# Seven block products in a down projection: a two-layer transformer trunk on TensorE

## The chip, the cores and the metric

The kernel runs on one core of a Trainium2 chip. The metric is the device time of one execution in microseconds (us). Before the change the median of three runs is 2252.79 us (2252.79 to 2252.91). The profile is of one more execution.

The engines by the profile's names: PE is TensorE (matmuls), PEld its loading of stationary operands, DVE is VectorE, ACT is ScalarE, POOL is GpSimd, SP is SyncE, whose queue carries the DMA transfers.

## The reference

The input is 256 tokens by 2048 features, in float32. Each of two layers does, with weights of its own:

```python
h = rms_norm(x, pre_mix_norm[l])
m = hybrid_mixer(h, l, w_in[l], w_o[l], ...)      # two kinds of attention, 8 heads each
x = x + rms_norm(m, post_mix_norm[l])
h = rms_norm(x, pre_ffn_norm[l])
f = (silu(h @ w_gate) * (h @ w_up)) @ w_down      # 2048 -> 5632 -> 2048
x = x + rms_norm(f, post_ffn_norm[l])
```

All weights together are some 400 MB, each used once per execution.

## The kernel before, in words

**Precision.** A float32 matmul is made of three matmuls in fp32r: each operand is split into a rounded part `hi` and a rest `lo`, and hi x hi, hi x lo and lo x hi are summed in PSUM. One matmul is a stationary 128 x 128 block (tokens) against 128 x 512 columns of weights.

**Weights.** They come in a fixed list `stream` of transfers of 512 KB, each a *K pair*: two blocks of 128 rows by 512 columns, in a tile `raw` (4 buffers). `feed` (L167) splits each: ScalarE rounds `hi` (L177), VectorE subtracts for `lo` (L179), 6 buffers each, up to LOOKAHEAD = 4 transfers ahead of their use.

**Gate and up.** Eleven chunks of 512 columns, each over 8 K pairs. For 5 of the 8, the two blocks of tokens (t), two of K and the two matrices (gate and up) give 8 block products, 24 matmuls. For pairs 2, 4 and 6 (in the first chunk 4 and 6) a 2 x 2 by 2 x 2 block product is made with 7 products, 21 matmuls. For that, `mixed_weights` (L145) makes four sums of weight blocks (L151, tiles `T`) on VectorE, rounds them on ScalarE (L160, `Th`), subtracts on VectorE (L162, `Tl`), and also splits one plain block (b22, L155 and L156). The tokens' sums (`token_sums`, L703 to L716: two `f` of hi + lo, four small sums `s`, a rounded `sh` on ScalarE and a rest `sl`) are made once per layer, for all three pairs, ahead of the first chunk's K loop. Four PSUM banks hold the chunk's results (`c`); four more hold products that several results share (`p`, `q`). These are added on VectorE at the chunk's end (L779 to L791), then silu and the product; the result is transposed on TensorE some ticks later (`flip`) into tiles `act`.

**Down.** Two halves of the output columns, each two blocks of 512 (c). The K loop has 22 pairs; a pair is two transfers, one for each c, and 24 matmuls (L840, L841, L843) into four banks `dn`. `prep` (L814) splits the pair's activations into `jh` (ScalarE, L820) and `jl` (VectorE, L822), up to two pairs ahead. In half 1 the last 3 pairs (TAIL) are done per t and c (L862 to L864), so that the first tokens finish early. `evac_chunk` (L363) squares a bank on ScalarE for the norm (L365) and multiplies it with the gain on VectorE (L369); `rescale` (L371) makes the factor and updates x (L377). In layer 0 `transposed` (L290) then makes the next layer's input `xI`; in layer 1 the result is stored.

**Order.** A scheduler fixes each engine's order of instructions when the kernel is built, from the program's order, priorities (URGENT for the evacuation) and data dependences. At run time an engine takes its list in that order and waits for semaphores. `tick` counts steps of the program; generators such as `flip` and the attention advance on ticks. Tiles live in pools; a pool that is released gives its room to later ones, whose first writers wait for the last readers.

Of the kernel before, what the change touches and what calls it, by code (L numbers as in the profile page):

```python
# [9 lines left out]
F32 = mybir.dt.float32  # L10
F32R = mybir.dt.float32r
# [6 lines left out]
P = 128  # L18
# [19 lines left out]
FIRST_ORDER = (0, 1, 3, 2, 4, 5, 6, 7)  # L38

# [12 lines left out]
def kernel(  # L52
# [51 lines left out]
    for l in range(L):  # L104
# [102 lines left out]
    rows0 = const.tile([32, P], F32, name="rows0")  # L207
    rows = const.tile([64, P], F32, name="rows")
# [23 lines left out]
    lams = const.tile([P, 4, L * 64], F32, name="lams")  # L232
    negones = const.tile([P, P], F32, name="negones")
# [6 lines left out]
    def late_constants():  # L240
# [18 lines left out]
        lprod = const.tile([P, 2, L * 64], F32, name="lprod")  # L259
        lsum = const.tile([P, 2, L], F32, name="lsum")  # L260
# [53 lines left out]
    def x_tiles(nm):  # L314
        return [wpool.tile([P, 2, S], F32R, tag="xT", bufs=KT, name=f"{nm}_{k}") for k in range(KT)]
# [47 lines left out]
    def evac_chunk(pool, acc, mg, ssm, gpost, c, t, nm, mpool=None):  # L363
        junk = pool.tile([P, CW], F32, tag="t2", name=f"jm_{nm}_{t}_{c}")
        nc.scalar.activation(junk, acc, AF.Square, accum_out=ssm[t][:, c : c + 1])  # L365
        if c % 2 == 0:
            mg[t, c // 2] = (mpool or pool).tile([P, 2, CW], F32, tag="qk", bufs=4, name=f"mg_{nm}_{t}_{c}")
# [206 lines left out]
    def mixer_in(pool, l, rs, xT, mix, mixed):  # L574
        st = None
        for n, c in enumerate(plan[l]["chunks"]):
# [21 lines left out]
            if n == 0:  # L598
                if l == 0:
                    with tc.issue_after(marks[0].ins), tc.issue_after(marks[1].ins), in_turn():  # L600
                        late_constants()
                        rs = [inv_rms(t, pool, "in0") for t in range(NT)]
# [38 lines left out]
    def load_gain(pool, v, nm):  # L641
# [3 lines left out]
        return gp  # L645

    xT = None
    for l in range(L):
# [52 lines left out]
        def token_sums(kp):  # L701

# [4 lines left out]
            a11, a21, a12, a22 = f[:, 0, 0:P], f[:, 0, P:S], f[:, 1, 0:P], f[:, 1, P:S]  # L707
            s = pool.tile([P, 4, P], F32, tag="t2", name=f"s{l}_{kp}")
            nc.vector.tensor_tensor(out=s[:, 0, :], in0=a21, in1=a22, op=ALU.subtract)
            nc.vector.tensor_tensor(out=s[:, 1, :], in0=s[:, 0, :], in1=a11, op=ALU.subtract)  # L710
            nc.vector.tensor_tensor(out=s[:, 2, :], in0=a11, in1=a21, op=ALU.subtract)
            nc.vector.tensor_tensor(out=s[:, 3, :], in0=s[:, 1, :], in1=a12, op=ALU.add)
            sh = gu.tile([P, 4, P], F32R, tag="sh", bufs=len(SEVEN), name=f"sh{l}_{kp}")
            nc.scalar.activation(sh, s, AF.Copy)
            sl = gu.tile([P, 4, P], F32R, tag="sl", bufs=len(SEVEN), name=f"sl{l}_{kp}")
            nc.vector.tensor_tensor(out=sl, in0=s, in1=sh.bitcast(F32), op=ALU.subtract)  # L716
            forms[kp] = (sh, sl)

        def product(a, stat, moving, first, last):
            sh, sl = stat  # L720
            hi, lo = moving
            nc.tensor.matmul(a, sh, hi, start=first, stop=False)  # L722
            nc.tensor.matmul(a, sh, lo, start=False, stop=False)  # L723
            nc.tensor.matmul(a, sl, hi, start=False, stop=last)  # L724
# [11 lines left out]
        def seven(banks, extra, c, kp, first, last):  # L736
# [3 lines left out]
            sh, sl = forms[kp]  # L740
            s1, s2, s3, s4 = ((sh[:, j, :], sl[:, j, :]) for j in range(4))
            p1, p6, p7, q5 = extra
            todo = (
                (p1, (e[:, 0, 0:P], e[:, 1, 0:P]), (hi[:, 0, :], lo[:, 0, :]), first, last),
                (banks[0], (o[:, 0, 0:P], o[:, 1, 0:P]), (hi[:, 1, :], lo[:, 1, :]), False, False),
                (q5, s1, m["t1"], first, last),
                (p7, s3, m["t3"], first, last),
                (p6, s2, m["t2"], first, last),
                (banks[1], s4, m["b22"], False, False),
                (banks[2], (o[:, 0, P:S], o[:, 1, P:S]), m["t4"], False, False),  # L750
            )
            for n, job in enumerate(todo):
                if n % 2 == 0:
                    tick()
                product(*job)

        for c in range(FF // CW):
# [3 lines left out]
            if c == 0:  # L761
# [3 lines left out]
                for kp in SEVEN:  # L765
                    token_sums(kp)
                order = order[2:]
            extra = None
            for kp in order:
# [6 lines left out]
                if kp == mine[-1]:  # L776
                    p1, p6, p7, q5 = extra
                    w = [pool.tile([P, CW], F32, tag="t2", name=f"w{j}_{l}_{c}") for j in range(4)]
                    nc.scalar.copy(w[0], p1)  # L779
                    nc.vector.tensor_tensor(out=w[1], in0=p6, in1=w[0], op=ALU.add)  # L780
                    nc.vector.tensor_tensor(out=w[2], in0=p7, in1=w[1], op=ALU.add)
                    nc.vector.tensor_tensor(out=w[1], in0=q5, in1=w[1], op=ALU.subtract)
                    nc.vector.tensor_tensor(out=w[3], in0=q5, in1=w[2], op=ALU.subtract)  # L783
# [18 lines left out]
        gu.release()  # L802
        dn = tc.alloc_tile_pool(name=f"dn{l}", bufs=4, reuse_waits="tile")
# [108 lines left out]
```

## Time and profile before

| | |
|---|---|
| median of three runs | 2252.79 us |
| profiled execution | 2252.42 us |
| its span (first to last instruction) | 2250.7 us |
| TensorE | 10210 matmuls and transposes, busy 99% |
| VectorE, ScalarE | busy 72%, 54% |
| transfers | 421.62 MB, 187 GB/s over the span |

In layer 0, gate and up run from about 420 to 887 us and down from 887 to 1128 us. Layer 1's first gate/up chunk is near 1550 us, and its last matmul begins at 2241.87 us.

A row of a timeline has the start, the duration, the engine, the line, the operation, output <- inputs, shapes and a count; in brackets the idle time before it and what ended it. Busy times of matmuls overlap, since a new one starts before the last has left the pipe: the distance between starts is the price of one. The same holds for VectorE, whose rows back to back overlap by some 0.09 us.

### The profile page before, as it was taken

To read this page: it belongs to the slowest core of one execution; us is meant where nothing else is said; L and a number is where in the kernel's file an instruction comes from. 1 tells how busy PE (TensorE), PEld (TensorE's weight loads), DVE (VectorE), ACT (ScalarE), POOL (GpSimd) and SP (SyncE) were. 2 spreads that over 40 slices of the span, in tenths; PEclk is the share of its full clock that TensorE was granted. 3 is DMA by queue.
4 is the path that set the end of the run, shared out by engine and by line. 5 is a ranking of instruction groups with operands and counts; after the bars stand their busy time and mean duration, and the time that the engine had idled before them with its cause. 6 is when DMAs were issued, how large, how long until landed. Compare 5 with 4: busy or idle time off the path is not lost.

```text
span 2250.7 us, 28018 instructions
## 1 busy us (share of the span) xinstructions
PE 2225.4 (99%) x10210; PEld 1833.5 (81%) x10210; DVE 1626.3 (72%) x2225; ACT 1222.4 (54%) x1834; POOL 37.6 (2%) x76
## 2 busy tenths in 40 slices
PE   8999999999999999999999999999999999999998
PEld 6888888788888888888887888887888888888886
DVE  6666555899989988555576665559998998975555
ACT  6545555665555546444465555546655555554443
POOL 1010000000000000000010000000000000000000
PEclk9999999999999999999999999999999999999999
DMA  7555555475665666556565555554666566565553
GB/s 238 180 169 163 163 182 184 127 229 187 204 206 188 199 209 208 189 188 204 171 195 175 162 167 161 186 186 141 205 200 209 190 199 205 190 218 192 191 198 135
DMA packets 216699, 421.62 MB, mean 187 GB/s; under 512 B 13200, under 2 KB 13808, under 8 KB 216048
## 3 DMA queue, kind: packets, MB, share of 16 engines
q1 hardware_dynamic: 216560, 419.83, 58.2%
q8 instruction: 80, 1.31, 0.2%
q14 instruction: 59, 0.48, 0.1%
HBM read 417.68 MB, written 2.10 MB: 187 GB/s over the span
## 4 chain that ended last, share of the span: by engine, by line
PE 92%; DVE 3%; ACT 2%; DMA 2%; issue 0%; POOL 0%; SPq 0%; DVEq 0%; ACTq 0%
PE c L722 10%; PE c L723 10%; PE c L724 10%; PE in L358 8%; PE in L360 7%; PE in L359 7%; PE dn L843 7%; PE dn L840 7%; PE dn L841 7%; PE o L360 2%; PE o L358 2%; PE o L359 2%; PE p L724 2%; PE p L723 2%; PE p L722 2%; DVE lo L179 1%
## 5 line engine op out<-in xcount | busy, mean ns | idle before, releaser
L179 DVE TENSOR_TENSOR lo<-raw,hi 128x1024 fp32r<-128x1024 f32 x720 | 873.6, 1227 | 329.8 <-ACT hi L177 324.5
L177 ACT ACTIVATE hi<-raw 128x1024 fp32r<-128x1024 f32 x720 | 749.5, 1056 | 469.1 <-PE in L360 166.5
L722 PE MATMUL c<-hi,xF 128*128 128x512 f32 x960 | 377.8, 394 | 2.0 <-DVE w L783 1.6
L724 PE MATMUL c<-hi,xF 128*128 128x512 f32 x960 | 374.2, 391 | 0.0
L723 PE MATMUL c<-lo,xF 128*128 128x512 f32 x960 | 373.6, 390 | 0.0
L840 PE MATMUL dn<-hi,jh 128*128 128x512 f32 x656 | 255.6, 390 | 0.0
L841 PE MATMUL dn<-lo,jh 128*128 128x512 f32 x656 | 255.2, 389 | 0.0
L722 PEld LDWEIGHTS c<-hi,xF 128*128 128x128 f32 x960 | 180.6, 188 | 39.1 <-DVE w L783 2.5
L724 PEld LDWEIGHTS c<-hi,xF 128*128 128x128 f32 x960 | 180.4, 188 | 37.8
L723 PEld LDWEIGHTS c<-lo,xF 128*128 128x128 f32 x960 | 180.5, 188 | 36.3
L843 PE MATMUL dn<-hi,jl 128*128 128x512 f32 x656 | 202.1, 389 | 0.0
L160 ACT ACTIVATE Th<-T 128x1024 fp32r<-128x1024 f32 x128 | 135.2, 1056 | 116.9 <-DVE T L151 106.5
L822 DVE TENSOR_TENSOR jl<-act,jh 128x512 fp32r<-128x512 f32 x88 | 60.7, 692 | 161.6 <-ACT jh L820 159.3
L820 ACT ACTIVATE jh<-act 128x512 fp32r<-128x512 f32 x88 | 55.0, 631 | 219.3 <-PE dn L841 213.5
L162 DVE TENSOR_TENSOR Tl<-T,Th 128x1024 fp32r<-128x1024 f32 x128 | 156.2, 1220 | 1.0 <-ACT Th L160 0.3
L358 PE MATMUL in<-hi,xT 128*128 128x512 f32 x384 | 155.3, 405 | 1.3 <-ACT hi L177 1.3
L358 PE MATMUL in<-hi,xI 128*128 128x512 f32 x384 | 154.0, 401 | 0.0
L359 PE MATMUL in<-lo,xT 128*128 128x512 f32 x384 | 150.7, 392 | 0.6 <-DVE lo L179 0.6
L360 PE MATMUL in<-hi,xT 128*128 128x512 f32 x384 | 150.8, 393 | 0.0
L359 PE MATMUL in<-lo,xI 128*128 128x512 f32 x384 | 149.9, 390 | 0.3 <-DVE lo L179 0.3
L360 PE MATMUL in<-hi,xI 128*128 128x512 f32 x384 | 150.2, 391 | 0.0
L841 PEld LDWEIGHTS dn<-lo,jh 128*128 128x128 f32 x656 | 123.1, 188 | 25.6
(247 smaller groups left out, 3224.0 us busy)
## 6 DMA issues: line engine op xcount, KB each, us to landing
raw<-in_w_in_dram SPq DMA_DIRECT2D x192, 512.0 KB, 3.8
raw<-in_w_gate_dram SPq DMA_DIRECT2D x176, 512.0 KB, 3.9
raw<-in_w_up_dram SPq DMA_DIRECT2D x176, 512.0 KB, 4.5
raw<-in_w_down_dram SPq DMA_DIRECT2D x176, 512.0 KB, 4.3
raw<-in_w_o_dram SPq DMA_DIRECT2D x64, 512.0 KB, 4.1
x<-in_x_dram SPq DMA_DIRECT2D x4, 512.0 KB, 7.6
gpost_mix<-in_post_mix_norm_dram SPq DMA_DIRECT2D x2, 1024.0 KB, 7.8
gpost_ffn<-in_post_ffn_norm_dram SPq DMA_DIRECT2D x2, 1024.0 KB, 7.2
```

The source lines that it names most:

```text
L162: nc.vector.tensor_tensor(out=tl, in0=sums[j], in1=th.bitcast(F32), op=ALU.subtract)
L177: nc.scalar.activation(hi, raw, AF.Copy)
L179: nc.vector.tensor_tensor(out=lo, in0=raw, in1=hi.bitcast(F32), op=ALU.subtract)
L358: nc.tensor.matmul(a, sh, hi[:, kk, :], start=first and kk == 0, stop=False)
L359: nc.tensor.matmul(a, sh, lo[:, kk, :], start=False, stop=False)
L360: nc.tensor.matmul(a, sl, hi[:, kk, :], start=False, stop=last and kk == 1)
L722: nc.tensor.matmul(a, sh, hi, start=first, stop=False)
L723: nc.tensor.matmul(a, sh, lo, start=False, stop=False)
L724: nc.tensor.matmul(a, sl, hi, start=False, stop=last)
L840: nc.tensor.matmul(accs[c, t], sh, hi[:, kk, :], start=first, stop=False)
L841: nc.tensor.matmul(accs[c, t], sh, lo[:, kk, :], start=False, stop=False)
L843: nc.tensor.matmul(accs[c, t], sl, hi[:, kk, :], start=False, stop=last)
```

## The change

**Down projection.** `DOWN_SEVEN` names 6 of the 22 K pairs of each half: 2, 5, 8, 11, 14, 17. For these, both transfers of the pair go through `mixed_weights` (its lines are now L151 to L167), the tokens' sums are made from `act` in `prep`, and 21 matmuls replace 24. The 2 x 2 blocks are tokens by K, and K by the two column blocks c. Four more PSUM banks hold the shared products; after pair 17 `shared_part` adds them into tiles `mg`, and `evac_sum` adds a finished bank to its part before the square and the product with the gain. Before, ScalarE squared the bank itself.

**Room.** Tiles T, Th and Tl of the down projection lie where the transposed input (`xT`, `xF`) of the phase before lay; the next layer's tiles `xI` are allocated after half 1's last seven pair. Constants needed only for setting up lie in a pool that is released early.

**First gate/up chunk.** The tokens' sums of pairs 4, 6 and 2 are made ahead of the K pairs 2, 5 and 7 of the first chunk, instead of all before its K loop (`FORM_AT`, by position in the loop).

```diff
+FORM_AT = {1: 4, 3: 6, 5: 2}
+DOWN_SEVEN = (2, 5, 8, 11, 14, 17)
...
+                if kp in DOWN_SEVEN:
+                    sevens.add(lay["down"][2 * half + 1, kp])
...
+    def new_x_pool(nm):
+        if x_pool[0] is not None:
+            x_pool[0].release()
+        x_pool[0] = tc.alloc_tile_pool(name=nm, bufs=1, side="right", reuse_waits="tile")
+        return x_pool[0]
...
+    def evac_sum(pool, acc, mg, ssm, gpost, c, t, nm):
+        m = mg[t, c // 2][:, c % 2, :]
+        nc.vector.tensor_tensor(out=m, in0=acc, in1=m, op=ALU.add)
+        junk = pool.tile([P, CW], F32, tag="t2", name=f"jm_{nm}_{t}_{c}")
+        nc.scalar.activation(junk, m, AF.Square, accum_out=ssm[t][:, c : c + 1])
+        nc.vector.tensor_tensor(out=m, in0=m, in1=gpost[:, c * CW : (c + 1) * CW], op=ALU.mult)
...
+    def seven_products(banks, extra, sums, a11, a12, a22, hi, lo, m, first, last):
+        s1, s2, s3, s4 = sums
+        p1, p6, p7, q5 = extra
+        todo = (
+            (p1, a11, (hi[:, 0, :], lo[:, 0, :]), first, last),
+            (banks[0], a12, (hi[:, 1, :], lo[:, 1, :]), False, False),
+            (q5, s1, m["t1"], first, last),
+            (p7, s3, m["t3"], first, last),
+            (p6, s2, m["t2"], first, last),
+            (banks[1], s4, m["b22"], False, False),
+            (banks[2], a22, m["t4"], False, False),
+        )
+        for n, job in enumerate(todo):
+            if n % 2 == 0:
+                tick()
+            product(*job)
+
+    def shared_part(extra, w):
+
+        p1, p6, p7, q5 = extra
+        nc.scalar.copy(w[0], p1)
+        nc.vector.tensor_tensor(out=w[1], in0=p6, in1=w[0], op=ALU.add)
+        nc.vector.tensor_tensor(out=w[2], in0=p7, in1=w[1], op=ALU.add)
+        nc.vector.tensor_tensor(out=w[1], in0=q5, in1=w[1], op=ALU.subtract)
+        nc.vector.tensor_tensor(out=w[3], in0=q5, in1=w[2], op=ALU.subtract)
...
-                for kp in SEVEN:
-                    token_sums(kp)
...
-            for kp in order:
+            for n, kp in enumerate(order):
+                if c == 0 and n in FORM_AT:
+                    pair_sums(FORM_AT[n])
...
+        mix_pool[0] = new_x_pool(f"sums{l}")
...
+                if kp in DOWN_SEVEN:
+                    a11, a12, a21, a22 = src[:, 0, 0:P], src[:, 1, 0:P], src[:, 0, P:S], src[:, 1, P:S]
+                    forms[kp] = token_sums(pool, dn, 2, a11, a12, a21, a22, f"{l}_{half}_{kp}")
...
+            def down_seven(kp):
+                for n in range(3):
+                    prep(kp + n)
+                jh, jl = split[kp]
+                a11, a12, a22 = ((jh[:, kk, cols], jl[:, kk, cols]) for kk, cols in ((0, slice(0, P)), (1, slice(0, P)), (1, slice(P, S))))
+                hi, lo = weights(plan[l]["down"][cc[0], kp], LOOKAHEAD)
+                m = weights(plan[l]["down"][cc[1], kp], LOOKAHEAD)
+                seven_products(got, extra, forms[kp], a11, a12, a22, hi, lo, m, kp == DOWN_SEVEN[0], kp == DOWN_SEVEN[-1])
...
+                if kp == DOWN_SEVEN[-1]:
+                    for t in range(NT):
+                        mg[t, half] = dn.tile([P, 2, CW], F32, tag="qk", bufs=4, name=f"mg_d{l}_{t}_{half}")
+                    shared_part(extra, [mg[t, half][:, j, :] for t in range(NT) for j in range(2)])
...
-                        evac_chunk(pool, accs[c, t], mg, ssm, gpost, c, t, f"d{l}", dn)
+                        evac_sum(pool, accs[c, t], mg, ssm, gpost, c, t, f"d{l}")
```

**How the order moves.** In all, TensorE's list is 72 rows shorter, VectorE's grows from 2180 to 2473 rows and ScalarE's from 1644 to 1720. Three places matter for what follows; in their rows the numbers behind a name tell tiles apart.

VectorE before the first seven pair of layer 0's first gate/up chunk; `lo_3868` is that pair's first rest, and `f`, `s`, `sl` belong to the tokens' sums of pairs 2, 4 and 6. Before:

```order
L706 TENSOR_TENSOR f_6_3854<-xF_13_3257 128x256
L716 TENSOR_TENSOR sl_2_3840<-s_2_3833,sh_2_3838 128x512
L716 TENSOR_TENSOR sl_4_3852<-s_4_3845,sh_4_3850 128x512
L709 TENSOR_TENSOR s_6_3857<-f_6_3854 128x128
L711 TENSOR_TENSOR s_6_3857<-f_6_3854 128x128
L710 TENSOR_TENSOR s_6_3857<-s_6_3857,f_6_3854 128x128
L179 TENSOR_TENSOR lo_3868<-raw_3582,hi_3866 128x1024
L712 TENSOR_TENSOR s_6_3857<-s_6_3857,f_6_3854 128x128
L151 TENSOR_TENSOR T_0_3870<-raw_3582,raw_3607 128x512
L151 TENSOR_TENSOR T_0_3870<-raw_3607 128x512
```

Now (`lo_3839` is the same rest; the sums of pair 4 go on behind these rows):

```order
L183 TENSOR_TENSOR lo_3839<-raw_3589,hi_3837 128x1024
L300 TENSOR_TENSOR rsq_ffn_1_3762<-rsq_ffn_1_3762 128x1
L155 TENSOR_TENSOR T_0_3841<-raw_3589,raw_3614 128x512
L301 TENSOR_SCALAR rsq_ffn_1_3762<-rsq_ffn_1_3762 128x1
L155 TENSOR_TENSOR T_0_3841<-raw_3614 128x512
L302 TENSOR_TENSOR rs_ffn_1_3761<-rs_ffn_1_3761,rsq_ffn_1_3762 128x1
L155 TENSOR_TENSOR T_1_3842<-T_0_3841,raw_3614 128x512
L160 TENSOR_TENSOR lo_3848<-raw_3614,hi_3847 128x512
L155 TENSOR_TENSOR T_1_3842<-T_1_3842,raw_3589 128x512
L166 TENSOR_TENSOR Tl_0_3853<-T_0_3841,Th_0_3851 128x1024
L773 TENSOR_TENSOR f_4_3883<-xF_8_3259 128x256
L166 TENSOR_TENSOR Tl_1_3857<-T_1_3842,Th_1_3855 128x1024
```

The weights' part of the seven pair has moved ahead of all sums of tokens, and the sums of pairs 2 and 6 have moved away.

VectorE at the start of layer 0's down projection, from the `jl` of the third pair on. Before:

```order
L822 TENSOR_TENSOR jl_0_2_7749<-act_1_4470,jh_0_2_7747 128x512
L179 TENSOR_TENSOR lo_7755<-raw_7751,hi_7753 128x1024
L179 TENSOR_TENSOR lo_7761<-raw_7757,hi_7759 128x1024
L822 TENSOR_TENSOR jl_0_3_7789<-act_1_4470,jh_0_3_7787 128x512
L822 TENSOR_TENSOR jl_0_4_7829<-act_2_4829,jh_0_4_7827 128x512
```

Now (this third pair is the first seven):

```order
L680 TENSOR_TENSOR s_0_2_7746<-s_0_2_7746,act_1_4477 128x128
L183 TENSOR_TENSOR lo_7759<-raw_7755,hi_7757 128x1024
L682 TENSOR_TENSOR s_0_2_7746<-s_0_2_7746,act_1_4477 128x128
L155 TENSOR_TENSOR T_0_7763<-raw_7755,raw_7761 128x512
L155 TENSOR_TENSOR T_0_7763<-raw_7761 128x512
L686 TENSOR_TENSOR sl_0_2_7753<-s_0_2_7746,sh_0_2_7751 128x512
L155 TENSOR_TENSOR T_1_7764<-T_0_7763,raw_7761 128x512
L160 TENSOR_TENSOR lo_7770<-raw_7761,hi_7769 128x512
L155 TENSOR_TENSOR T_1_7764<-T_1_7764,raw_7755 128x512
L166 TENSOR_TENSOR Tl_0_7775<-T_0_7763,Th_0_7773 128x1024
L852 TENSOR_TENSOR jl_0_3_7807<-act_1_4477,jh_0_3_7805 128x512
L166 TENSOR_TENSOR Tl_1_7779<-T_1_7764,Th_1_7777 128x1024
```

Where one `lo` of 1024 columns stood, the four T, half a `lo`, `sl` and two Tl stand now, in front of the fourth pair's rests.

TensorE at the end of layer 0's down projection (`dn_3_1` is the last bank of down, `in_6` the first of the next layer's input projection, `x_68` the first 128 tokens). Before, where the first transposes (`xT_ps_0`) stand 20 rows ahead of these:

```order
L862 MATMUL dn_3_1_8648<-hi_9433,jh_1_21_9447 128x512
L863 MATMUL dn_3_1_8648<-lo_9435,jh_1_21_9447 128x512
L864 MATMUL dn_3_1_8648<-hi_9433,jl_1_21_9449 128x512
L296 MATMUL xT_ps_1_9525<-ident,x_68 128x128 x4
L862 MATMUL dn_3_1_8648<-hi_9433,jh_1_21_9447 128x512
L863 MATMUL dn_3_1_8648<-lo_9435,jh_1_21_9447 128x512
L864 MATMUL dn_3_1_8648<-hi_9433,jl_1_21_9449 128x512
L358 MATMUL in_6_0_9736<-hi_9437,xI_0_7719 128x512
```

Now:

```order
L919 MATMUL dn_3_1_8776<-hi_9712,jh_1_21_9726 128x512
L920 MATMUL dn_3_1_8776<-lo_9714,jh_1_21_9726 128x512
L310 MATMUL xT_ps_0_9791<-ident,x_68 128x128 x4
L921 MATMUL dn_3_1_8776<-hi_9712,jl_1_21_9728 128x512
L372 MATMUL in_6_0_10017<-hi_9716,xI_0_9680 128x512
L310 MATMUL xT_ps_1_9805<-ident,x_68 128x128 x4
L373 MATMUL in_6_0_10017<-lo_9718,xI_0_9680 128x512
L310 MATMUL xT_ps_2_9819<-ident,x_68 128x128 x4
```

Before, 50 of the 72 matmuls of the tail stood ahead of the first transposes and 22 behind; now 71 stand ahead and one behind, and the next layer's first matmul follows.

More of the change, by code (lines that the diff above doesn't have):

```diff
@@ L314, in x_tiles @@
     def x_tiles(nm):
-        return [wpool.tile([P, 2, S], F32R, tag="xT", bufs=KT, name=f"{nm}_{k}") for k in range(KT)]
+        return [x_pool[0].tile([P, 2, S], F32R, tag="xT", bufs=KT, name=f"{nm}_{k}") for k in range(KT)]
     def inv_rms(t, pool, nm):
@@ L706, in token_sums @@
                 nc.vector.tensor_tensor(out=f[:, kk, :], in0=st[:, 0, :].bitcast(F32), in1=st[:, 1, :].bitcast(F32), op=ALU.add)
[L707 to L724, printed above, removed]
+            forms[kp] = token_sums(pool, gu, len(SEVEN), f[:, 0, 0:P], f[:, 1, 0:P], f[:, 0, P:S], f[:, 1, P:S], f"{l}_{kp}")
         def eight(banks, c, kp, toks, first, last):
@@ L739, in seven @@
             e, o = xT[2 * kp], xT[2 * kp + 1]
[L740 to L755, printed above, removed]
+            a11, a12, a22 = (e[:, 0, 0:P], e[:, 1, 0:P]), (o[:, 0, 0:P], o[:, 1, 0:P]), (o[:, 0, P:S], o[:, 1, P:S])
+            seven_products(banks, extra, forms[kp], a11, a12, a22, hi, lo, m, first, last)
         for c in range(FF // CW):
@@ L843, in down @@
                             nc.tensor.matmul(accs[c, t], sl, hi[:, kk, :], start=False, stop=last)
+            def down_seven(kp):
[6 more added lines that the diff above has]
+                seven_products(got, extra, forms[kp], a11, a12, a22, hi, lo, m, kp == DOWN_SEVEN[0], kp == DOWN_SEVEN[-1])
             tail = TAIL if half == 1 else 0
             for kp in range(nkp - tail):
-                down(kp, range(NT))
+                if kp not in DOWN_SEVEN:
+                    down(kp, range(NT))
+                    continue
+                if kp == DOWN_SEVEN[0]:
+                    extra = four_banks(half, [f"{q}_d{l}_{half}" for q in ("p1", "p6", "p7", "q5")])
+                down_seven(kp)
+                if kp == DOWN_SEVEN[-1]:
+                    for t in range(NT):
+                        mg[t, half] = dn.tile([P, 2, CW], F32, tag="qk", bufs=4, name=f"mg_d{l}_{t}_{half}")
+                    shared_part(extra, [mg[t, half][:, j, :] for t in range(NT) for j in range(2)])
+            if half == 1:
+                xT = None
+                if l + 1 < L:
+                    new_x_pool(f"x{l + 1}")
+                    xT = x_tiles(f"xI{l}")
             for t in range(NT):
```

58 lines of the change are left out of this document (38 added, 20 removed).

## The prediction

> **What bounds the kernel now.** I read the page first, then tables of stages, then the waits of TensorE, then single rows. From the page:
>
> ```profile
> span 2250.7 us, 28018 instructions
> ...
> PE 2225.4 (99%) x10210; PEld 1833.5 (81%) x10210; DVE 1626.3 (72%) x2225; ACT 1222.4 (54%) x1834; POOL 37.6 (2%) x76
> ...
> PE 92%; DVE 3%; ACT 2%; DMA 2%; issue 0%; POOL 0%; SPq 0%; DVEq 0%; ACTq 0%
> ...
> L179 DVE TENSOR_TENSOR lo<-raw,hi 128x1024 fp32r<-128x1024 f32 x720 | 873.6, 1227 | 329.8 <-ACT hi L177 324.5
> ...
> L160 ACT ACTIVATE Th<-T 128x1024 fp32r<-128x1024 f32 x128 | 135.2, 1056 | 116.9 <-DVE T L151 106.5
> ...
> L822 DVE TENSOR_TENSOR jl<-act,jh 128x512 fp32r<-128x512 f32 x88 | 60.7, 692 | 161.6 <-ACT jh L820 159.3
> ...
> L162 DVE TENSOR_TENSOR Tl<-T,Th 128x1024 fp32r<-128x1024 f32 x128 | 156.2, 1220 | 1.0 <-ACT Th L160 0.3
> ```
>
> TensorE is busy 99% and 92% of the chain. A matmul's 0.39 us is its length in the pipe, not its price: the down projection starts like this.
>
> ```profile
> 887.17 0.39 PE L840 MATMUL dn<-hi,jh 128*128 128x512 f32 x1
> 887.40 0.39 PE L841 MATMUL dn<-lo,jh 128*128 128x512 f32 x1
> ...
> 892.61 0.39 PE L840 MATMUL dn<-hi,jh 128*128 128x512 f32 x1
> ```
>
> Between first and last row lie the 24 matmuls of one K pair: 5.44 us, so **0.2267 us** per matmul. The next table has, per window, the width and then the busy time of PE, PEld, DVE, ACT and POOL, the granted clock, the DMA share and GB/s. The first window lies in gate and up, where 3 of 8 K pairs are already done with seven products; the second in the down projection; the third is the worst stretch of the first gate/up chunk, and the last the slowest 3 us of it.
>
> ```profile
> 470.00:860.00 390.00, 390.00 (x1761) 323.16 (x1759) 349.94 (x412) 218.30 (x253) 0.00 (x0) 1.00 0.62 200
> 885.00:990.00 105.00, 105.00 (x469) 86.96 (x468) 63.28 (x66) 51.31 (x61) 0.00 (x0) 1.00 0.60 199
> ...
> 436.00:448.00 12.00, 8.68 (x29) 5.81 (x28) 11.72 (x18) 4.56 (x7) 0.00 (x0) 0.86 0.37 117
> ...
> 441.75:444.75 3.00, 3.00 (x6) 1.95 (x7) 3.00 (x5) 1.06 (x1) 0.00 (x0) 0.50 0.38 69
> ```
>
> In the down projection TensorE never waits, and VectorE is busy 60%: a matmul less is 0.2267 us less, as long as VectorE carries what replaces it. In gate and up VectorE is busy 349.94 of 390, 90%, and TensorE still does not wait. Only where all comes late does it wait:
>
> ```profile
> PE p L723 <- DVE lo L179: 3.6, 2, 1.8
> ...
> PE c L722 <- DVE w L783: 1.6, 2, 0.8
> ...
> PE q L722 <- ACT Th L160: 1.2, 2, 1.1
> ```
>
> These are the first chunks of the two layers.
>
> **Matmuls removed.** 6 pairs, 2 halves, 2 layers are 24 pairs, each with 21 matmuls in place of 24: 72 x 0.2267 = **16.3 us**, all on the path.
>
> **What VectorE gets instead.** Its rows back to back give prices by their starts:
>
> ```profile
> 721.30 0.69 DVE L151 TENSOR_TENSOR T<-T,raw 128x512 f32<-128x512 f32 x1
> 721.91 0.69 DVE L156 TENSOR_TENSOR lo<-raw,hi 128x512 fp32r<-128x512 f32 x1
> ...
> 723.11 1.22 DVE L162 TENSOR_TENSOR Tl<-T,Th 128x1024 fp32r<-128x1024 f32 x1
> 724.25 1.22 DVE L179 TENSOR_TENSOR lo<-raw,hi 128x1024 fp32r<-128x1024 f32 x1
> ...
> 437.38 0.28 DVE L709 TENSOR_TENSOR s<-f 128x128 f32<-128x128 f32 x1
> 437.58 0.28 DVE L711 TENSOR_TENSOR s<-f 128x128 f32<-128x128 f32 x1
> ```
>
> So 1.14 us for 1024 columns, 0.60 for 512, 0.20 for 128. A plain down pair costs two lo and one jl, 2.87 us. A seven pair costs one lo (1.14), four sums T (2.40), the half lo of b22 (0.60), two Tl (2.27), jl (0.60), four small token sums (0.80) and sl (0.60): 8.41. The pattern is two plain pairs and one seven: VectorE 14.15 us, TensorE 5.44 + 5.44 + 21 x 0.2267 = 15.64 us. That is 90%. By the groups' means (1.227, 0.69, 1.22, 0.28) instead of the starts it is 15.9, or 102%: these are the two ends. Nearest is gate and up: there the same starts give, per 8 pairs, 3 x 6.41 + 5 x 2.28 + ten steps of the evacuation at about 0.61 = 36.7 of 42.4 us (86.6%; 5 plain and 3 seven pairs and two groups of transposes), and the window shows 90% and no wait. The true load thus lies a few per cent above the starts (near 14.7 us here), and I take **0**. The other end costs 15.9 - 15.64 = 0.27 us a period, 24 x 0.27 = 6.5 us.
>
> ScalarE rounds two Th (1.06 each, from the page), half of hi and the sums sh in place of one hi:
>
> ```profile
> 434.55 1.06 ACT L177 ACTIVATE hi<-raw 128x1024 fp32r<-128x1024 f32 x1 [1.70 <-DMA raw<-in_w_up_dram]
> ...
> 439.44 0.63 ACT L714 ACTIVATE sh<-s 128x512 fp32r<-128x512 f32 x1 [2.79 <-DVE s L712]
> ```
>
> That is 2.11 + 0.6 + 0.63 - 1.06 = 2.3 us more per 15.64; from 49% (51.31 of 105) it goes to some 64%. DMA needs the same bytes in 3% less time, at a share of 0.60.
>
> **The start of a half.** The first seven comes third, when VectorE still has the last chunk's evacuation in front. Before, that ends at 889.82 (here the row is the jl of the third pair):
>
> ```profile
> 889.82 0.69 DVE L822 TENSOR_TENSOR jl<-act,jh 128x512 fp32r<-128x512 f32 x1
> ```
>
> From there, in the changed order, come jl 0.6, four small sums 0.8, lo 1.14, three T and sl 2.4, b22's lo and the fourth T 1.2, Tl 1.14: ready at 897.1. TensorE first uses it after two pairs and seven matmuls, at 887.17 + 10.88 + 1.59 = 899.6. The cover is 2.5 us, and the transposes of the last chunk's output add to it. In half 1, VectorE has four more adds from the evacuation; by the same count some 2 us are left. I take 0; without the cover it is up to 2 us at each of four places.
>
> **Evacuation.** The final sum needs an addition before the square. At the end of layer 1 nothing covers it:
>
> ```profile
> 2241.87 0.39 PE L864 MATMUL dn<-hi,jl 128*128 128x512 f32 x1
> 2242.29 0.60 ACT L365 ACTIVATE jm_d<-dn 128x512 f32<-128x512 f32 x1 [3.39 <-PE dn L864]
> ```
>
> One addition of 512 columns is put between these: 0.60 plus a handover of some 0.05, **+0.65 us**. Its other copies, and the 4 additions and a copy per half that form the shared part, lie beside matmuls.
>
> **The layer boundary.** Before, TensorE waits here twice:
>
> ```profile
> 1134.94 0.66 PE L296 MATMUL xT_ps<-ident,x 128*128 128x128 f32 x4 [0.29 <-DVE x L377]
> ...
> 1136.15 0.50 PE L359 MATMUL in<-lo,xI 128*128 128x512 f32 x1 [0.32 <-DVE lo L179]
> ```
>
> A group of transposes and its price, and that of a rounded rest of xI, follow from these rows (0.67 us with one matmul, so 0.44 alone; 0.86 for three, some 0.26 each at the starts):
>
> ```profile
> 427.23 0.60 PE L296 MATMUL xT_ps<-ident,x 128*128 128x128 f32 x4
> ...
> 427.90 0.40 PE L722 MATMUL c<-hi,xF 128*128 128x512 f32 x1
> ...
> 1137.74 0.86 DVE L304 SCALAR_TENSOR_TENSOR xI<-xT_ps,gains,xI 128x128 fp32r<-128x128 f32 x3
> ```
>
> In the changed order all but one of layer 0's down matmuls stand ahead of the first transposes, and the new layer's first matmul stands directly behind. It waits for ScalarE to round xI, about 0.6 us. Up to the ninth tile, VectorE has some 8.3 us of work (two lo, eleven xI, an addition, a product, an update of x and the small steps), while TensorE gets there after 26 matmuls, three groups of transposes and the 0.6: 7.8. So another 0.5, and some 0.9 at the next transposes. 2.0 less the 0.6 of before: **+1.4**, bounds 0 and +4.
>
> **First chunk.** Its token sums were three sets ahead of the first seven; now one. One set is two f (0.34), four small (0.20), one sl (0.60): 2.07 us. What it costs today:
>
> ```profile
> 435.65 0.39 PE L722 MATMUL p<-hi,xF 128*128 128x512 f32 x1
> 439.25 0.50 PE L723 MATMUL p<-lo,xF 128*128 128x512 f32 x1 [1.82 <-DVE lo L179]
> 441.75 0.80 PE L722 MATMUL q<-Th,sh 128*128 128x512 f32 x1 [1.07 <-ACT Th L160]
> 442.34 0.63 PE L722 MATMUL p<-Th,sh 128*128 128x512 f32 x1
> ...
> 474.85 0.39 PE L722 MATMUL p<-hi,xF 128*128 128x512 f32 x1
> ```
>
> Between the first and the last row are 138 matmuls and two groups of transposes: 31.28 + 0.88 = 32.2 us, taken 39.2, so 7 us are lost, among them 1.6 to slow matmuls (six in the 3 us at clock 0.50, where six at full pitch take 1.36). Upper bound of the gain: two sets, 4.1 us a layer. But the new order has other waits. ScalarE rounds the next pair's weights ahead of Th, and the last of these are rounded from 434.55 on, when their transfer has come; so Th comes to 436.7 and 437.6 and Tl to 439.3, and the sums of pair 4 stand behind both. Walked through with the prices above: waits of 0.6, 1.0, 0.5 and 0.5 up to the first q, 0.5 and 0.7 at pair 6, about 1 at the next chunk's first bank. That is 5 us without slow matmuls, some 6.5 with. I take 1.0 us saved in layer 0 and 0.5 in layer 1, **-1.5**; bounds +1 and -8.2 for both.
>
> [...] The window 436 to 448 has clock 0.86 with no wait above 1.82 us. [...]
>
> **Sum.** -16.3 + 0 + 0.65 + 1.4 - 1.5 = -15.75. The profiled execution took 2252.42 us (span 2250.7); the runs' median is 2252.79, 0.4 above. 2252.79 - 15.75 = **2237.0 us**.
>
> **Rivals.**
> *The first chunk gains its bound* (4.1 us a layer): -16.3 - 8.2 + 0.65 + 1.4, 2230.3. For it: VectorE is busy 11.72 of 12 us there. Against: Th now waits for ScalarE and for transfers.
> *VectorE decides in the sevens, at the groups' means*: 6.5 us back, 2243.5. For it: the token sums bring a handover to ScalarE and back in every seven, which gate and up have only in the first chunk. Against: the cover of 2.5 us at the start grows, since VectorE needs less per period than TensorE.
> *Slower than before.* The same handover makes Tl late in each seven, and the waits bring the slow matmuls of 441.75 along. Place: the third product. A seven that loses over 16.3 / 24 = 0.68 us has lost what it saved, so this decides from 16.3 us of VectorE per period (1.04 times the period). Price: 0.27 + 1.6 a seven, 24 x 1.87 = 45 us, 2282. Against: VectorE would have to be 11% slower than near 14.7.
> *The clock falls by the banks alone.* Seven products go to seven banks in turn. If this alone cost 1.6 us per seven, as the slow matmuls did, the time would be 2237 + 38 = 2275. The window 470 to 860 does the same with clock 1.00. [...]
> *The change doesn't shorten TensorE's work*, because the matmuls left would be spaced wider: about 2252. Against: the sevens of gate and up run at the same 0.2267.
>
> **How the numbers follow.** Forecast 0.68, first chunk's bound 0.13, VectorE at the means 0.10, slower by the handover 0.04, clock 0.01, no shorter 0.04. Low end of the range: 16.3 and 8.2 less, 0.65 more, no loss at the boundary: 2229. High end: VectorE at the means, boundary +4, no gain in the first chunk: 2252.8 - 16.3 + 6.5 + 0.65 + 4 = 2247.6; all at once is unlikely, so 2246. A measurement of this kernel tells 0.2% (4.5 us) from no change: faster below 2248.3. Faster 0.91, same 0.04, slower 0.05.
>
> **What would show it.** Right: 72 matmuls fewer; windows inside each half with TensorE busy throughout, clock 1.00, VectorE at 88 to 97%; the first chunk 37.5 to 39 us long; two or three waits below 1 us at the boundary; the last square 0.65 us behind an addition. Wrong: rows in the waits of TensorE in which dn, p or q of the down projection waits for Tl or sl, or a clock below 1.00 in these windows. A first wait of over 2 us at the start of a half would take my cover away, and a long wait for xI or lo behind layer 0 my estimate of the boundary.

## The result, and the profile after

The changed kernel takes 2271.23 us (median of 4 runs, 2269.62 to 2271.57) against 2252.85 us (2252.79 to 2253.2) for the kernel before beside it. The ratio is **1.0082**, 95% interval 1.007 to 1.0094: 18 us slower, where 16 us faster was predicted.

The page of the changed kernel: the span, the engines, and the two costliest groups of matmuls.

```profile
span 2269.3 us, 28211 instructions
...
PE 2244.4 (99%) x10138; PEld 1818.5 (80%) x10138; DVE 1775.4 (78%) x2521; ACT 1282.7 (57%) x1910; POOL 34.1 (2%) x76
...
L673 PE MATMUL c<-lo,xF 128*128 128x512 f32 x960 | 382.1, 399 | 1.4 <-DVE lo L183 1.3
L672 PE MATMUL c<-hi,xF 128*128 128x512 f32 x960 | 381.1, 398 | 0.7 <-ACT w L709 0.6
```

TensorE has 72 instructions fewer and is busy 19 us longer. The gate/up groups, whose number the change does not touch, have a mean of 398 and 399 ns, where it was 394 and 390:

```profile
L722 PE MATMUL c<-hi,xF 128*128 128x512 f32 x960 | 377.8, 394 | 2.0 <-DVE w L783 1.6
...
L723 PE MATMUL c<-lo,xF 128*128 128x512 f32 x960 | 373.6, 390 | 0.0
```

The waits of TensorE in the changed kernel do not explain it; these are the largest, beside those at the program's start and two of 1.3 us that were there before:

```profile
PE c L673 <- DVE Tl L166: 2.0, 3, 0.8
PE c L673 <- DVE lo L183: 1.3, 2, 0.7
...
PE xT_ps L310 <- DVE rsq_d_p L301: 1.1, 1, 1.1
```

No row has dn, p or q of the down projection waiting for anything. So the matmuls themselves are further apart. Two windows, gate and up and then the first half of down (columns as in the prediction):

```profile
470.00:860.00 390.00, 390.00 (x1715) 315.01 (x1714) 344.99 (x407) 216.14 (x247) 0.00 (x0) 1.00 0.60 195
900.00:1100.00 200.00, 200.00 (x883) 164.92 (x882) 186.83 (x264) 127.65 (x162) 0.00 (x0) 1.00 0.61 202
```

In the first window 1715 matmuls start where 1761 did, at the same clock of 1.00 and with TensorE never idle. The timeline shows the spacing:

```profile
599.71 0.39 PE L672 MATMUL c<-hi,xF 128*128 128x512 f32 x1
599.94 0.40 PE L673 MATMUL c<-lo,xF 128*128 128x512 f32 x1
...
602.27 0.40 PE L674 MATMUL c<-hi,xF 128*128 128x512 f32 x1
```

Eleven matmuls lie between the first and the last row: 0.2327 us each, not 0.2267. A seven pair in the down projection shows which of them are wide:

```profile
991.79 0.39 PE L672 MATMUL p_d<-hi,jh 128*128 128x512 f32 x1
...
993.15 0.40 PE L672 MATMUL q_d<-Th,sh 128*128 128x512 f32 x1
...
995.25 0.39 PE L672 MATMUL dn<-hi,sh 128*128 128x512 f32 x1
...
995.93 0.40 PE L672 MATMUL dn<-Th,jh 128*128 128x512 f32 x1
```

The six from hi and jh take 1.36 us (0.2267 each), the nine from Th and sh 2.10 (0.2333), the three from hi and sh 0.68 (0.2267). In gate and up it is those with xF, in the input projection those with xT or xI (0.2333 from 59.70 us on); the output projection, with mix, is spaced as before (0.227). The wide ones have one thing in common: one of the two operands lies in the room that the change made on the right.

### The profile page after: what moved, and what is told of

Its sections match the earlier page's. It is cut to its first block, busy times and chain, and to the rows that moved or that the text cites. A ratio compares the mean times of both kernels' runs of the same rounds, so it can differ in the third digit from the quotient of the medians.

```text
span 2269.3 us, 28211 instructions
## 1 busy us (share of the span) xinstructions
PE 2244.4 (99%) x10138; PEld 1818.5 (80%) x10138; DVE 1775.4 (78%) x2521; ACT 1282.7 (57%) x1910; POOL 34.1 (2%) x76
## 4 chain that ended last, share of the span: by engine, by line
PE 94%; DMA 2%; DVE 2%; ACT 1%; issue 0%; POOL 0%; DVEq 0%; SPq 0%; ACTq 0%
PE c L673 11%; PE c L672 11%; PE c L674 10%; PE in L372 8%; PE in L374 8%; PE in L373 7%; PE dn L874 5%; PE dn L875 5%; PE dn L877 5%; PE o L374 2%; PE o L373 2%; PE o L372 2%; PE p L673 2%; PE p L672 2%; PE p L674 2%; PE actT_ps L828 1%
## 5 line engine op out<-in xcount | busy, mean ns | idle before, releaser
L183 DVE TENSOR_TENSOR lo<-raw,hi 128x1024 fp32r<-128x1024 f32 x696 | 846.5, 1227 | 331.1 <-ACT hi L181 327.4
L181 ACT ACTIVATE hi<-raw 128x1024 fp32r<-128x1024 f32 x696 | 728.4, 1057 | 529.0 <-PE in L374 178.6
L164 ACT ACTIVATE Th<-T 128x1024 fp32r<-128x1024 f32 x176 | 185.7, 1056 | 135.7 <-DVE T L155 130.5
L166 DVE TENSOR_TENSOR Tl<-T,Th 128x1024 fp32r<-128x1024 f32 x176 | 215.1, 1222 | 7.9 <-ACT Th L164 7.7
L874 PE MATMUL dn<-hi,jh 128*128 128x512 f32 x464 | 180.8, 390 | 0.0
L875 PE MATMUL dn<-lo,jh 128*128 128x512 f32 x464 | 180.6, 389 | 0.0
L877 PE MATMUL dn<-hi,jl 128*128 128x512 f32 x464 | 142.9, 389 | 0.0
L155 DVE TENSOR_TENSOR T<-T,raw 128x512 f32<-128x512 f32 x176 | 121.2, 688 | 1.2
L874 PEld LDWEIGHTS dn<-hi,jh 128*128 128x128 f32 x464 | 87.1, 188 | 18.3
L875 PEld LDWEIGHTS dn<-lo,jh 128*128 128x128 f32 x464 | 87.1, 188 | 18.2
```

The source lines that it names most:

```text
L166: nc.vector.tensor_tensor(out=tl, in0=sums[j], in1=th.bitcast(F32), op=ALU.subtract)
L181: nc.scalar.activation(hi, raw, AF.Copy)
L183: nc.vector.tensor_tensor(out=lo, in0=raw, in1=hi.bitcast(F32), op=ALU.subtract)
L874: nc.tensor.matmul(accs[c, t], sh, hi[:, kk, :], start=first, stop=False)
L875: nc.tensor.matmul(accs[c, t], sh, lo[:, kk, :], start=False, stop=False)
L877: nc.tensor.matmul(accs[c, t], sl, hi[:, kk, :], start=False, stop=last)
```

## The experiments

The built programs give each tile's start. In bytes per partition, and the remainder of 256:

```
                          before          changed kernel
raw, first of 4           26208  (96)      21568  (64)
hi, first of 6            75360  (96)      37952  (64)
mix, first of 16         124512  (96)      87104  (64)
sh, gate and up          181856  (96)     177216  (64)
xT, xF, xI, first of 16   42592  (96)     196576 (224)
Th in down                    -           204768 (224)
```

The sizes of all these tiles are multiples of 512, so all tiles of a pool share a remainder of 256. Before, all pools stood in one row behind the constants. The change took 4640 bytes of constants out of that row, which moved the left pools, and put xT on the right, which ends at a fixed address.

**Theory A:** a matmul takes longer when its two operands' starts differ in a small remainder. **Rival B:** the place on the right is slow. **Rival C:** VectorE's and ScalarE's heavier traffic widens the spacing.

### A shift of 32 bytes, in both directions

```diff
+    pad = const.tile([P, 8], F32, name="pad")
+    nc.gpsimd.memset(pad, 0.0)
     eps = const.tile([P, 1], F32, name="eps")
```

This is the changed kernel with its left pools 32 bytes further on.

> The changed kernel with one more constant of 32 bytes per partition, which moves every tile of the left pools (raw, hi, lo, act, jh, sh, ...) by 32 bytes; the room of xT, xF, xI and of the sums on the right stays where it is. Theory A (start addresses): in the changed kernel left tiles begin at a multiple of 64 bytes and the right room begins 32 behind one; a matmul whose moving operand and whose neighbour's stationary operand differ in this takes 0.2334 us instead of 0.2267. With all at the same remainder: 5168 + 240 such matmuls x 6.7 ns = 36 us less, about 2235. Rival B (the place): the upper end of the memory is slower to read whatever the remainder; then it stays at 2271. Rival C: the wider spacing has to do with VectorE's and ScalarE's heavier traffic; also 2271.

Measured: 2265.08 us, ratio 1.0059 (1.0044 to 1.0074). Some 5 us came back, not 36: theory A in its first form, with the remainder of 64, fell, or B held. The other direction told more: the kernel before, with nothing changed but this.

```diff
+        if nm == "xT0":
+            nc.gpsimd.memset(wpool.tile([P, 8], F32, tag="pad0", name="pad0"), 0.0)
+        tiles = [wpool.tile([P, 2, S], F32R, tag="xT", bufs=KT, name=f"{nm}_{k}") for k in range(KT)]
+        if nm == "xT0":
+            nc.gpsimd.memset(wpool.tile([P, 8], F32, tag="pad1", name="pad1"), 0.0)
+        return tiles
```

> The kernel before with a pad of 32 bytes ahead of the room of xT, xF and xI and one behind, so that these tiles begin at a multiple of 64 and all others 32 behind one; nothing else moves by more than 64 bytes. Theory A: the matmuls with xT, xF or xI (some 5300) take 0.2334 instead of 0.2267 us, 35 us more: about 2288. Rivals B and C: no change, 2253.

Measured: 2282.4 us, ratio 1.0135 (1.012 to 1.015): 30 us for 32 bytes. Its windows:

```profile
470.00:860.00 390.00, 390.00 (x1720) 315.87 (x1719) 343.45 (x401) 216.49 (x247) 0.00 (x0) 1.00 0.61 196
900.00:1100.00 200.00, 200.00 (x888) 165.59 (x887) 118.18 (x123) 97.60 (x122) 0.00 (x0) 1.00 0.60 198
```

Gate and up, with xF, is as slow as in the changed kernel; the down projection, whose matmuls read no tile that was shifted against another, is not. Its window before the change:

```profile
900.00:1100.00 200.00, 200.00 (x886) 165.65 (x885) 114.21 (x114) 95.00 (x119) 0.00 (x0) 1.00 0.58 192
```

In this run raw starts at the remainder 96 and hi, lo, jh and jl at 160, so a difference from raw, which the transfers write, costs the down projection nothing: 888 matmuls start in this window, 886 did before. The room is at its old place and VectorE has nothing more to do, so B and C are not needed for this effect.

### All starts at one remainder

With 32 bytes of pad the left pools had the remainder 96 of 256, the right room 224. The next run makes them equal up to 2048.

```diff
+    pad = const.tile([P, 232], F32, name="pad")
+    nc.gpsimd.memset(pad, 0.0)
```

> The changed kernel with a pad of 928 bytes instead of 32, so that all tiles of the left pools and of the room on the right begin at the same remainder of 2048 (2016), as all did before the change (1632). The 32-byte pad made only the remainders of 64 and 128 equal (those of 256 differ by 128) and saved 6 us of 36; the shift of 32 bytes in the kernel before cost 30 us. Theory A, now with a larger unit (256 to 2048): matmuls with xT, xF, xI go back to 0.2267, about 30 us less than the 32-byte pad: 2235. Rival B (the upper end is slow whatever the remainder): stays at 2265.

Measured: **2235.88 us**, ratio 0.9933 (0.9918 to 0.9948). The room is still on the right, VectorE does all that the change gives it, and the time is 16 us below that of before. B and C fall. Its windows:

```profile
470.00:860.00 390.00, 390.00 (x1756) 322.71 (x1755) 352.07 (x414) 219.71 (x251) 0.00 (x0) 1.00 0.63 202
900.00:1100.00 200.00, 200.00 (x884) 165.62 (x883) 184.36 (x254) 124.02 (x157) 0.00 (x0) 1.00 0.62 207
```

1756 matmuls again in the first, where the changed kernel had 1715.

### How large the unit is

Three more pads in the changed kernel. The same two lines with 488, 168 and 104 words, for differences of 1024, 256 and 512 between left and right:

```diff
+    pad = const.tile([P, 488], F32, name="pad")
```

> The changed kernel with a pad of 1952 bytes: the left pools and the room on the right have the same remainder of 1024 but differ by 1024 in that of 2048. If the unit is 1024 or less (theory A with 256, 512 or 1024): as with the pad of 928, about 2235. If 2048 counts: about 2265. By rival B: 2265.

```diff
+    pad = const.tile([P, 168], F32, name="pad")
```

> The changed kernel with a pad of 672 bytes: the left pools and the room on the right have the same remainder of 256 but differ by 256 in that of 512. So far: a difference of 32 (the change as it is, and the shift in the kernel before) or of 128 is slow, none and 1024 are fast. If the unit is 256 or less, 2236; if it is 512 or more, about 2265.

```diff
+    pad = const.tile([P, 104], F32, name="pad")
```

> The same with a pad of 416 bytes: equal remainders of 512, a difference of 512 in that of 1024. If the unit is 512 or less, 2236; if it is 1024, about 2265. With the run before, it gives the unit.

And in the kernel before, xT shifted by 64 bytes against tiles whose remainder of 256 stays:

```diff
+            nc.gpsimd.memset(wpool.tile([P, 16], F32, tag="pad0", name="pad0"), 0.0)
...
+            nc.gpsimd.memset(wpool.tile([P, 48], F32, tag="pad1", name="pad1"), 0.0)
```

> The kernel before with the room of xT, xF and xI moved by 64 bytes and the tiles behind it by 256 (pads of 64 and 192 bytes). All tiles but xT, xF, xI keep their remainder of 256; these differ by 64. If the unit found is 256 and any difference in it costs the same, as 32 (30.5 us here) and 128 did: about 2282. If differences that are a multiple of 64 cost nothing at this place: 2252.

| difference modulo 256, the smaller way round | kernel | us | ratio to before |
|---|---|---|---|
| 32 | before, xT shifted by 32 | 2282.4 | 1.0135 (1.012 to 1.015) |
| 64 | before, xT shifted by 64 | 2283.07 | 1.0141 (1.0124 to 1.0158) |
| 96 | changed, no pad | 2271.23 | 1.0082 (1.007 to 1.0094) |
| 128 | changed, pad of 32 | 2265.08 | 1.0059 (1.0044 to 1.0074) |
| 0 | changed, pad of 928 | 2235.88 | 0.9933 (0.9918 to 0.9948) |
| 0 (256 of 512) | changed, pad of 672 | 2236.12 | 0.993 (0.9916 to 0.9943) |
| 0 (512 of 1024) | changed, pad of 416 | 2236.42 | 0.9931 (0.9918 to 0.9945) |
| 0 (1024 of 2048) | changed, pad of 1952 | 2236.65 | 0.993 (0.9914 to 0.9947) |

All four differences that are no multiple of 256 are slow, all four that are one are fast, and the slow ones are found at two places of the room. Each of the four was measured one way round only. The window of the shift by 64 counts 1719 matmuls, that of the shift by 32 1720:

```profile
470.00:860.00 390.00, 390.00 (x1719) 316.25 (x1719) 344.66 (x403) 216.44 (x246) 0.00 (x0) 1.00 0.61 196
```

### Is it the difference, or the remainder itself?

The kernel before with everything moved, so that all tiles have the remainder that the changed kernel's left pools have.

```diff
+    pad = const.tile([P, 120], F32, name="pad")
+    nc.gpsimd.memset(pad, 0.0)
```

> The kernel before with 480 bytes more ahead of all pools, so that all tiles begin at the remainder 64 of 1024 that the changed kernel's left pools have (before: 608). They stay equal among themselves. If only the difference between two operands counts: 2252, no change. If the remainder itself counts (in the changed kernel's gate and up, the products with Th and sh were wider too, 232 ns, though both lie in the left pools): some 600 matmuls or more at 5 ns, 2255 and above, and up to 2290 if it holds for all.

Measured: 2251.64 us, ratio 1.0 (0.9991 to 1.0009). A common shift costs nothing. It is the difference.

One thing is left open. In the changed kernel's gate and up, Th, Tl, sh and sl all lie in the left pools with one remainder, and yet:

```profile
610.39 0.40 PE L672 MATMUL q<-Th,sh 128*128 128x512 f32 x1
...
612.47 0.39 PE L672 MATMUL c<-hi,sh 128*128 128x512 f32 x1
```

Nine matmuls in 2.08 us, 0.2311 each. In the kernel before and in the one with the pad of 928 bytes they take 0.2267. The pairing of one matmul's two operands alone does not explain these; what they have beside them that differs was not found. There are 64 such groups of nine in all; at 4.4 ns a matmul that is 2.5 us of the 34.

Nor is it only a matmul's own operands that count. The stationary operand of the next one is loaded (PEld) while a matmul runs:

```profile
612.92 0.40 PE L674 MATMUL c<-hi,sl 128*128 128x512 f32 x1
612.92 0.19 PEld L672 LDWEIGHTS c<-Th,xF 128*128 128x128 f32 x1
613.16 0.39 PE L672 MATMUL c<-Th,xF 128*128 128x512 f32 x1
```

Here hi and sl agree, and the xF loaded meanwhile differs. By the starts in nanoseconds such a matmul takes 237 ns, where it took 227 before. But in the kernel before with xT shifted by 64 bytes the same pair takes 226 ns, so a rule for single matmuls does not follow from these runs; the sum over a whole kernel does.

### The parts of the change, one by one

The one-by-one token sums alone, in the kernel before:

```diff
-                for kp in SEVEN:
-                    token_sums(kp)
...
+            for n, kp in enumerate(order):
+                if c == 0 and n in FORM_AT:
+                    token_sums(FORM_AT[n])
```

> The kernel before with only the token sums of the first gate/up chunk made one by one (FORM_AT). All addresses keep their remainder. My prediction gave 1.5 us for it, with bounds +1 and -8.2: 2251.3. The changed kernel's trace has waits of 0.81, 0.67 and 0.34 us in layer 0's first chunk and no slow clock; by that it saves about 3 us a layer: 2247.

Measured: 2248.55 us, ratio 0.9985 (0.9976 to 0.9995): 3.3 us less, by the interval 1.1 to 5.4. Its trace shows where. From the first matmul of the first chunk's p to that of the next chunk's, layer 0 takes 37.46 us in place of 39.20 and layer 1 36.70 in place of 38.38. The reverse, in the changed kernel with the 32-byte pad:

```diff
+                for kp in SEVEN:
+                    pair_sums(kp)
...
-                if c == 0 and n in FORM_AT:
-                    pair_sums(FORM_AT[n])
```

> The padded kernel of the first run, but with the token sums of all three pairs ahead of the first chunk's K loop again, as before the change. Against the first run this costs what the one-by-one order saves: 1.5 us by my prediction, about 6 us by the changed kernel's trace. If theory A holds for the first run: 2236.5 or 2241; if not, 2273 to 2277.

Measured: 2270.46 us, ratio 1.0083 (1.0068 to 1.0098), 5.4 us more than its neighbour at 2265.08. Its worst stretch of the first chunk:

```profile
441.00:453.00 12.00, 9.12 (x26) 6.06 (x25) 12.00 (x18) 4.62 (x6) 0.00 (x0) 0.72 0.40 130
```

The clock falls to 0.72 here. The longest waits are the old ones:

```profile
PE p L675 <- DVE lo L183: 3.6, 2, 1.8
```

With the sums one by one, in the kernel with the pad of 928, the clock stays at 1.00, though three waits of 0.5 to 0.8 us stand in 4 us; the window and the rows:

```profile
435.00:445.00 10.00, 7.98 (x33) 5.62 (x32) 8.72 (x14) 4.89 (x7) 0.00 (x0) 1.00 0.57 172
```

```profile
437.24 0.50 PE L674 MATMUL c<-Th,xF 128*128 128x512 f32 x1 [0.51 <-ACT Th L164]
...
439.02 0.50 PE L675 MATMUL c<-Tl,xF 128*128 128x512 f32 x1 [0.82 <-DVE Tl L166]
...
440.90 0.50 PE L675 MATMUL c<-lo,xF 128*128 128x512 f32 x1 [0.68 <-DVE lo L183]
```

The amount of waiting does not decide it, though. In the run with the one-by-one sums in the kernel before, the same stretch has less of it (1.7 of 10 us, the longest wait 0.82), and the clock falls:

```profile
435.00:445.00 10.00, 8.31 (x27) 5.74 (x27) 8.84 (x15) 4.85 (x7) 0.00 (x0) 0.83 0.60 187
```

Of the executions profiled, the five with the sums ahead have a clock of 0.91 to 0.96 over the first chunk, in both layers. Of the nine with the sums one by one, seven have 1.00 in both layers; two, this one and the pad of 1952 bytes, have 0.95 in layer 0. What sets these two apart is not known.

Then the kernel with the pad of 928 bytes ("the run before" in what was expected) without seven products in the down projection. It keeps two small edits of the down loop, a second tick per step and another order of the four banks:

```diff
-DOWN_SEVEN = (2, 5, 8, 11, 14, 17)
+DOWN_SEVEN = ()
...
-                        evac_sum(pool, accs[c, t], mg, ssm, gpost, c, t, f"d{l}")
+                        evac_chunk(pool, accs[c, t], mg, ssm, gpost, c, t, f"d{l}", dn)
```

> The run before with no seven pairs in the down projection (and the old evacuation): the new room, the one-by-one sums and the pad stay. What the sevens alone are worth is this less that run. By my prediction 16.3 - 0.65 - 1.4 = 14.2 us: 2249 by theory A (where the one-by-one sums are worth 3 us, 2249.5), 2279 by rival B. If the sevens bring no more than 5 us, VectorE's load is a loss of its own.

Measured: 2248.76 us, ratio 0.9986 (0.9977 to 0.9996). The sevens alone are worth 2248.76 - 2235.88 = **12.9 us**.

### One seven more per half

```diff
-DOWN_SEVEN = (2, 5, 8, 11, 14, 17)
+DOWN_SEVEN = (2, 5, 7, 10, 12, 15, 17)
```

> The changed kernel with the pad of 928 bytes and seven instead of six pairs with seven products per half (2, 5, 7, 10, 12, 15, 17). 12 matmuls fewer: 2.7 us less, 2233.2, if VectorE still carries it: by its starts it then has 25.4 us of work in 25.8 (3 plain pairs and 2 sevens), and by the window of the run with the pad (184.36 of 200 us) some 2 to 4% more than the starts. If VectorE is the bound there, TensorE waits and the time is 2236 or above.

Measured: 2236.03 us over 5 runs, ratio 0.9932 (0.9918 to 0.9945): no better than six. The window shows VectorE at 96%, with no wait of TensorE; the gain goes in the tail of half 1, where two kinds of wait are new:

```profile
900.00:1100.00 200.00, 200.00 (x884) 165.51 (x883) 192.06 (x273) 129.25 (x163) 0.00 (x0) 1.00 0.61 201
```

```profile
PE dn L922 <- DVE lo L183: 1.7, 2, 0.9
...
PE dn L921 <- ACT hi L181: 0.9, 1, 0.9
```

Together 2.6 us, against 12 x 0.2267 = 2.7 saved. That VectorE has no lead left behind pair 17 is how I read these waits for `lo`; no run changed it alone.

## Why the prediction was wrong

**The step that failed** is one that the sum did not have. The prediction took 0.2267 us for the matmuls that were removed, and left the price of the 9160 others of 512 columns where it was. Its rival that "the matmuls left would be spaced wider" had 0.04 and was dismissed with the seven products of gate and up, which had always lain in the same row of pools. The part of the change under **Room** was not costed at all. It moved xT, xF, xI and the down projection's T, Th and Tl to starts that differ from those of hi, lo, jh and sh by 160 modulo 256 (96 the other way round). The sum measured for that: the ratios 1.0082 and 0.9933 are 0.0149 of 2252 apart, **34 us**. By the spacing: 5872 matmuls now have operands that differ, where 16 had before; at 0.2327 instead of 0.2267, as in the eleven above, that is 35.

The profile before does hold this price, in a few rows that the prediction did not read. Of its 9232 matmuls of 512 columns, 16 read a constant, negtri, as stationary operand; it starts at the remainder 0, where hi, xT and ah_sb start at 96:

```profile
241.87 0.40 PE L360 MATMUL in<-hi,xT 128*128 128x512 f32 x1
242.11 0.39 PE L476 MATMUL za_sb<-ah_sb,negtri 128*128 128x512 f32 x1
242.34 0.28 PE L477 MATMUL za_sb<-ah_sb,negone 128*128 128x256 f32 x1
```

By the starts in nanoseconds the first of these takes 236 ns and the second 232. In the run with all pools moved, where the difference from negtri is 64, they take 226 and 229. The starts are also in the built program, and that the change moved the operand of more than half of all matmuls could be read in the diff.

**The rest of the sum held**, as the kernel with the pad of 928 bytes shows:

| term | predicted | measured |
|---|---|---|
| 72 matmuls | -16.3 | -16.3 by spacing: 0.2267 again |
| VectorE's load | 0 | no wait in down; window at 92% (184.36 of 200) |
| evacuation at the end | +0.65 | +0.73 |
| layer boundary | +1.4 | +1.7 |
| first chunks | -1.5 | -3.3 (in the kernel before) |
| sum without the moved room | -15.75 | -16.0 (2251.91 to 2235.88) |

The measured terms add up to -17.2, the whole is -16.0, and no term explains the 1.2 between them. That the whole comes so near to the forecast is in part luck: the first chunks gained 1.8 more than forecast, the end and the boundary cost 0.4 more, and the unexplained 1.2 took most of the rest.

The end and the boundary in the same kernel:

```profile
2224.20 0.39 PE L923 MATMUL dn<-hi,jl 128*128 128x512 f32 x1
2224.63 0.69 DVE L389 TENSOR_TENSOR mg_d<-dn,mg_d 128x512 f32<-128x512 f32 x1 [0.33 <-PE dn L923]
2225.35 0.63 ACT L391 ACTIVATE jm_d<-mg_d 128x512 f32<-128x512 f32 x1 [1.78 <-DVE mg_d L389]
```

```profile
1118.25 0.51 PE L374 MATMUL in<-hi,xI 128*128 128x512 f32 x1 [0.70 <-ACT xI L315]
...
1125.94 0.66 PE L312 MATMUL xT_ps<-ident,x 128*128 128x128 f32 x4 [0.83 <-DVE rsq_d_p L303]
...
1127.13 0.50 PE L375 MATMUL in<-lo,xI 128*128 128x512 f32 x1 [0.54 <-DVE lo L183]
...
1131.57 0.51 PE L376 MATMUL in<-hi,xI 128*128 128x512 f32 x1 [0.24 <-DVE xI L320]
```

The square starts 1.15 us behind the last matmul's start, where it was 0.42. The waits at the boundary are 2.3 us in place of 0.6; 2.0 were predicted, with the first for ScalarE's xI as the walk had it. Two small terms were estimates of mine that no row shows: 0.05 for the handover, where here the addition ends 0.03 ahead of the square, and 0.6 for the first xI, where the wait is 0.70.

**The sevens** brought 12.9 us, where the walk had 16.3 - 0.65 - 1.4 = 14.2. With the measured end and boundary it is 13.9; the remaining 1 us is within the spread of the runs of the two kernels (2247.04 to 2249.87 and 2235.52 to 2239.14).

**VectorE as the bound** of the sevens, the rival with 0.10 and the one on the slower side with 0.04, did not come at six pairs: no row of the down projection waits, so the cover at a half's start held, and the busy share was within the 88 to 97% forecast. At seven pairs per half waits came, in the tail and not at the third product.

**The first chunk** was a term mis-sized, by half: 3.3 us instead of 1.5. The interval of that run holds both, but the 1.7 us that its trace shows in each layer do not fit the 1.0 and 0.5 of the forecast. The walk itself was near. In the kernel with the pad of 928 bytes layer 0's first chunk takes 37.0 us, 4.8 above the 32.2 at full pitch, where the walk had 5 without slow matmuls; four waits came (0.51, 0.82, 0.68 and one of 0.61 for the next chunk's first bank), where it had seven. What it had too large is the price of slow matmuls, which came in layer 0 of two executions out of nine. The sum of the waits does not decide whether they come: 1.7 of 10 us went along with a clock of 0.83, and 2.0 of 10 with 1.00. Nor does the longest one: the clock fell behind waits of at most 1.8 us with the sums ahead and of at most 0.82 us with the sums one by one, and with 0.82 it also stayed at 1.00. What makes the clock fall stays open.

## What to carry to other kernels

Where a change moves a pool, list the starts of both operands of the costliest matmuls before and after, and compare their remainders of 256; a difference cost 2.6 to 2.9% of a matmul in the stretches above (0.2327 and 0.2333 us against 0.2267), at full clock and without a wait. Only the count per window, the starts and the busy time of TensorE showed it. Price an edit's allocations like its instructions, and when busy time grows with fewer instructions, look at the distance between starts first. A pad of 928 bytes made a change that lost 18 us into one that gains 16.

## What the runs showed of the hardware

- In these kernels fp32r matmuls of 128 x 128 by 128 x 512 follow each other after 0.2267 us where the starts of all moving and stationary operands agree modulo 256 bytes, and after 0.2327 to 0.2333 us in the stretches above where they do not. Whole runs lose about the same for differences of 32, 64 and 96 bytes (30, 31 and 34 us); for 128 it was some 5 us less. The groups of nine at 0.2311 us, whose own operands agree, are not explained.
- A common shift of all tiles changes nothing (ratio 1.0, 0.9991 to 1.0009).
- Moving xT, xF and xI, the stationary operands of their matmuls, by 32 bytes against the moving ones cost 30 us (2282.4 against 2251.88), with the clock at 1.00 and TensorE never idle from 470 to 860 us, where 1720 matmuls start in place of 1761. What in the hardware makes the difference count, and whether an access of another engine takes part, no run here shows.
